# A two-layer encoder trunk on one core: the beginning put into a written order behind products of zeros, a mixer's normalisation moved by two steps, and another last block

## The chip, the cores and the metric

The kernel runs on one core of one Trainium2 chip. Its time is the device time of one execution in microseconds (us). PE is TensorE with its weight loads as PEld, DVE is VectorE, ACT is ScalarE, POOL is GpSimd, SP is SyncE, which issues most DMAs.

## What is computed

512 tokens of 1024 channels pass two layers. Layer 0 mixes by a short gated convolution beside latent attention, which share one input projection; layer 1 by a convolution module (gate, depthwise convolution of width 31, LayerNorm, swish, projection). Each layer ends with a squared-ReLU MLP of hidden width 4096. Every sub-layer is wrapped in two RMS norms:

```python
x = x + rms_norm(m, g[1])
h = rms_norm(x, g[2])
x = x + rms_norm(squared_relu_mlp(h, mlp_w1[i], mlp_w2[i]), g[3])
```

## The kernel before

Activations lie with channels on the 128 partitions, so 1024 channels are eight chunks of 128 x 512 tokens. Products are in float32 split in two float32r parts, a high part (`hi`) and what is left of it (`lo`): each product of a chunk is three matmuls, hi*hi, hi*lo and lo*hi, and one 128-column block of an output (a **block** below) is 24 of them into one PSUM bank. Weights come in **strips** of 128 x 1024: `strip` (line 210) loads one (SP), ACT casts its high part `whi` (L223), POOL subtracts to get `wlo` (L224). A strip passes through one of two raw buffers (more in later phases) into one of eight pairs of `whi` and `wlo`. PSUM has eight banks: three named `S`, two `pj`, one `o`, two `mi`.

The **beginning** (`START`, `split_x`, lines 564 to 600): for each chunk of x, SP loads it, DVE scales it by its gain (L572), ACT rounds it to `h` (L230), DVE subtracts the low part (L233). ACT squares the chunks (L358), DVE adds the squares (L333), PE sums them over partitions (L368), DVE makes the reciprocal root in 14 small instructions (`rstd`, L394 to L424), PE spreads it over the partitions (`spread`, L433) and ACT puts it into `R0` (L600). Only with `R0` can DVE empty a block's bank (L608). Five blocks (`latent`) need it, twelve and one more follow. Here the framework's scheduler orders all engines. The first transfer of all is `gtok`, a row of gains for the last norm, on the ACT queue (L1133).

From layer 0's MLP on (`M2`) the tokens go in two halves, A and B, and a list of steps is the program: `up` and `down` are the MLP's two products, `pw1` and `pw2` the convolution module's, `norm` its LayerNorm, `join` a residual with its norms. The numbers of a step are layer, quarter of the hidden width, and first and last block. DVE runs in the order in which the steps are issued; the scheduler orders the other engines. The convolutions are DVE instructions (L832) that `fill(us)` puts between the steps, as many as the step's worth in `FILL` pays. Steps of a chain (`norm`, `join`) are long runs of dependent instructions, and `hold` and `pace` put steps of the other half between them, taken from the list until one of the same half comes. `norm A` first uses up what is left of A's convolutions, a step for each 1.96 us of them; then it takes the mean (L847), subtracts it (L856), squares and adds (L333), makes the root, spreads it, multiplies (L864), and ACT applies the swish and rounds to `h`, on which `pw2 A` waits.

The **end** (`end_step`): the last two 128-token blocks b of half B are made with tokens on partitions, in two halves f of 512 channels; the last bank (b 1, f 1) in two parts of 256 columns. `piece` adds what was kept (L1029), squares on ACT with a sum (L1031), multiplies by the gain on POOL (L1032); `root` adds the sums and runs `rstd`; `leave` does the last multiply-add (L1051) and stores.

Of the kernel before, what the change touches and what calls it, by code (L numbers as in the profile page):

```python
# [37 lines left out]
OP_US, STEP_US = 0.39, 2.35  # L40
TAP_US = {T // 2: (0.395, 0.525)}
FILL = {'up': 2.3, 'down': 2.3, 'first': 2.6, 'sum': 1.8, 'pw1': 4.8, 'pw2': 2.3}
START = ['x', (128,), 'x', (256, 512, 768), 'x', 'x', 'x', 'x', 'x', 'x', ()]
ADD0 = 0
LAG = 4
MULT_POOL = (0, 0, 0, 0, 0, 0, 0, 3)
W0 = True
WHOLE = (True,) * 5
# [82 lines left out]
def trunk(ctx: ExitStack, tc: tile.TileContext, a, out: bass.AP, out_b: bass.AP):  # L131
# [310 lines left out]
    def gains(layer, n):  # L442
        return V_GAIN + (layer * 4 + n) * NC
# [123 lines left out]
    s0 = Sum(NC, FULL, nc.gpsimd if ADD0 else nc.vector, whole=W0)

    def split_x(j):
        load_x(xs[j], j)  # L570
        t, (hi, lo) = scratch(T), (h.t[:, :T] for h in hs[j])
        nc.vector.tensor_scalar(out=t, in0=xs[j].t, scalar1=col(gains(0, 0) + j), scalar2=None, op0=ALU.mult)  # L572
        settle()
        split((hi, lo), t, nc.vector, late=late)
        if j >= LAG:
            s0.square(xs[j - LAG].t)

    win, j = [], 0
    for what in START:
        if what == "x":  # L580
            split_x(j)
            j += 1
        else:
            win.append(strip(a["win"][len(win)], cuts=what))
    nc.sync.dma_start(kst, a["consts"])
    nc.sync.dma_start(vec[:, V_QN:], a["vecs"][:, V_QN:])
    settle()
    for j in range(NC - LAG, NC):
        s0.square(xs[j].t)
        settle()  # L590
# [9 lines left out]
    nc.scalar.activation(R0, spread(rstd(s0.done(STARTS), D, inverse=inv0)[:, :NB]), AF.Copy)  # L600


    def latent(m0, n, gain, slot):
        lat, ss = [], Sum(n, FULL, whole=WL)
        for j in range(n):
            acc = linear(win[m0 + j] if m0 + j < len(win) else strip(a["win"][m0 + j]), hs)
# [408 lines left out]
    def end_step(tok, h, layer, g):  # L1015

        f12 = lack.pop(h)
        banks_step(h, g)
        ws = []
        for k in range(NC):  # L1020
            ws.append(take())
            issue([turn_mm(turned[0, f][0], h, ws[k], k, 0, slice(0, T), f * T) for f in range(2)])
            settle()
        parts = {b: [] for b in range(2)}

        def piece(b, f, cols):
            acc, m, _ = turned[b, f]
            acc, m, g = acc[:, cols], m[:, cols], turned["gain"][:, f * T + cols.start : f * T + cols.stop]
# [6 lines left out]
        def root(b):  # L1035
            s = misc()[:, :1]
            p = parts[b]
            if len(p) == 3:
                nc.vector.scalar_tensor_tensor(
                    out=s, in0=p[0], scalar=p[1], in1=p[2], op0=ALU.add, op1=ALU.add  # L1040
                )
            else:
                nc.vector.tensor_tensor(out=s, in0=p[0], in1=p[1], op=ALU.add)
            return rstd(s, D, tuple(f[:, b : b + 1] for f in f12))

        def leave(b, r, n):
            w = T // n
            for f in range(2):
                for i in range(n):
                    m, x = (t[:, i * w : i * w + w] for t in turned[b, f][1:])  # L1050
                    nc.vector.scalar_tensor_tensor(  # L1051
                        out=x, in0=m, scalar=r, in1=x, op0=ALU.mult, op1=ALU.add
                    )
                    q = nc.scalar if i % 2 else nc.sync
                    q.dma_start(out_b[b * P : (b + 1) * P, f * T + i * w : f * T + i * w + w], x)
# [204 lines left out]
```

## Time and profile before

| | |
|---|---|
| three runs, median | 1172.47 us (1171.79 to 1172.93) |
| the profiled execution's own time | 1173.47 us |
| its span, first to last instruction | 1171.7 us |
| PE busy | 1134.6 us (97%) |
| POOL, ACT, DVE busy | 846.0, 661.5, 649.2 us |
| mean granted TensorE clock | 0.993 |

The span is 1.8 us shorter than the execution's time; the rest is start and stop around it. A share of busy time is a mean over stages, so PE's idle time is best looked for stage by stage.

### The profile page before, as it was taken

What the parts mean: (1) busy time and instruction counts of PE and PEld (TensorE: products, weight loads), DVE (VectorE), ACT (ScalarE), POOL (GpSimd) and SP (SyncE); (2) the same over time, 40 slices, a digit from 0 to 9 for tenths busy, and PEclk for the clock granted to TensorE, in tenths of its full rate; (3) what the DMA queues carried; (4) which work ended last, traced back from release to release, by engine and by line L of the source; (5) the groups of instructions that cost most, each with busy time, mean ns of one, the idle gap of its engine ahead of it and who ended that gap; (6) DMA issues with size and microseconds to landing.
All of it is one profiled execution on the core that took longest, in us unless ns stands there. A gap on an engine that the chain in (4) does not pass through costs nothing.

```text
span 1171.7 us, 22121 instructions
## 1 busy us (share of the span) xinstructions
PE 1134.6 (97%) x8492; PEld 1081.3 (92%) x8492; DVE 649.2 (55%) x1693; ACT 661.5 (56%) x1211; POOL 846.0 (72%) x408
## 2 busy tenths in 40 slices
PE   7999989999999999999999999999999999999996
PEld 5778778999999999999999999999999999898895
DVE  5672699455432222669996364589995254131134
ACT  5431677456744445744655686745566776455451
POOL 5663563148878778688898578789787878779881
PEclk9999999999999999999999899999999999999999
DMA  6421332027545555545565355556555545565530
GB/s 222 154 90 30 106 100 72 1 92 235 201 161 182 178 180 169 174 163 181 180 216 187 122 196 181 179 171 207 169 195 178 180 163 180 165 231 182 179 108 36
DMA packets 55257, 184.47 MB, mean 157 GB/s; under 512 B 6384, under 2 KB 10352, under 8 KB 55152
## 3 DMA queue, kind: packets, MB, share of 16 engines
q1 hardware_dynamic: 54576, 182.02, 46.9%
q8 instruction: 66, 1.08, 0.4%
q10 hardware_dynamic: 576, 1.05, 0.3%
q14 instruction: 39, 0.32, 0.1%
HBM read 180.94 MB, written 2.10 MB: 156 GB/s over the span
## 4 chain that ended last, share of the span: by engine, by line
PE 85%; DVE 6%; ACT 3%; DMA 3%; POOL 1%; issue 1%; SPq 0%; DVEq 0%; ACTq 0%; POOLq 0%
PE S L246 20%; PE S L247 19%; PE S L248 19%; PE pj L246 5%; PE pj L247 5%; PE pj L248 5%; PE pj L990 4%; PE S L990 4%; DMA raw<-in_win 2%; POOL wlo L224 1%; ACT whi L223 1%; DVE pr L767 1%; DMA raw<-in_w 1%; PE mi L433 1%; PE mi L770 1%
## 5 line engine op out<-in xcount | busy, mean ns | idle before, releaser
L224 POOL TENSOR_TENSOR wlo<-raw,whi 128x1024 fp32r<-128x1024 f32 (+2 forms) x347 | 802.0, 2327 | 263.2 <-ACT whi L223 243.6
L223 ACT ACTIVATE whi<-raw 128x1024 fp32r<-128x1024 f32 (+2 forms) x347 | 356.6, 1033 | 368.7 <-PE S L247 173.3
L246 PE MATMUL S<-h,whi 128*128 128x256 f32 (+3 forms) x1208 | 347.7, 291 | 5.0 <-ACT h L230 2.9
L247 PE MATMUL S<-h,whi 128*128 128x256 f32 (+3 forms) x1208 | 349.0, 290 | 0.0
L248 PE MATMUL S<-h,wlo 128*128 128x256 f32 (+3 forms) x1208 | 348.7, 289 | 0.0
L246 PEld LDWEIGHTS S<-h,whi 128*128 128x128 f32 x1208 | 229.0, 191 | 10.1 <-ACT h L230 3.4
L247 PEld LDWEIGHTS S<-h,whi 128*128 128x128 f32 x1208 | 230.5, 191 | 3.5 <-issue 0.2
L248 PEld LDWEIGHTS S<-h,wlo 128*128 128x128 f32 x1208 | 230.5, 191 | 3.3 <-POOL wlo L224 0.3
L832 DVE SCALAR_TENSOR_TENSOR pj<-u,taps,pj 128x256 f32<-128x256 f32 x464 | 192.6, 484 | 1.3
L246 PE MATMUL S<-hid,whi 128*128 128x256 f32 (+2 forms) x664 | 185.3, 281 | 1.4 <-DVE acc L333 1.2
L248 PE MATMUL S<-hid,wlo 128*128 128x256 f32 (+2 forms) x664 | 186.5, 282 | 0.0
L247 PE MATMUL S<-hid,whi 128*128 128x256 f32 (+2 forms) x664 | 186.3, 281 | 0.0
L246 PEld LDWEIGHTS S<-hid,whi 128*128 128x128 f32 x664 | 124.8, 189 | 2.5 <-DVE acc L333 1.8
L248 PEld LDWEIGHTS S<-hid,wlo 128*128 128x128 f32 x664 | 125.3, 189 | 0.0
L247 PEld LDWEIGHTS S<-hid,whi 128*128 128x128 f32 x664 | 125.3, 189 | 0.0
L246 PE MATMUL pj<-h,whi 128*128 128x256 f32 (+3 forms) x344 | 105.5, 307 | 9.5 <-ACT h L230 7.6
L248 PE MATMUL pj<-h,wlo 128*128 128x256 f32 (+3 forms) x344 | 105.3, 306 | 0.3 <-POOL wlo L224 0.3
L247 PE MATMUL pj<-h,whi 128*128 128x256 f32 (+3 forms) x344 | 105.3, 306 | 0.0
L246 PEld LDWEIGHTS pj<-h,whi 128*128 128x128 f32 x344 | 65.5, 191 | 12.4 <-ACT h L230 7.6
L236 DVE TENSOR_TENSOR hid<-S,hid 128x256 fp32r<-128x256 f32 (+2 forms) x102 | 42.9, 420 | 52.7 <-ACT hid L230 52.2
L247 PEld LDWEIGHTS pj<-h,whi 128*128 128x128 f32 x344 | 65.5, 190 | 3.4 <-DVE h L233 1.1
L248 PEld LDWEIGHTS pj<-h,wlo 128*128 128x128 f32 x344 | 65.6, 191 | 3.1 <-POOL wlo L224 0.7
(267 smaller groups left out, 1740.2 us busy)
## 6 DMA issues: line engine op xcount, KB each, us to landing
raw<-in_w SPq DMA_DIRECT2D x224, 512.0 KB, 3.3
raw<-in_pw SPq DMA_DIRECT2D x48, 512.0 KB, 3.3
raw<-in_w2t SPq DMA_DIRECT2D x32, 512.0 KB, 3.3
raw<-in_win SPq DMA_DIRECT2D x16, 512.0 KB, 3.3
x<-in_xT SPq DMA_DIRECT2D x16, 256.0 KB, 4.4
raw<-in_wout SPq DMA_DIRECT2D x8, 512.0 KB, 3.3
raw<-in_wq SPq DMA_DIRECT2D x8, 192.0 KB, 2.4
out<-x SPq DMA_DIRECT2D x8, 128.0 KB, 3.5
```

The costliest lines, as they stand in the source:

```text
L223: nc.scalar.activation(h, r, AF.Copy)
L224: nc.gpsimd.tensor_tensor(out=lo[:, c0:c1], in0=r, in1=h.bitcast(F32), op=ALU.subtract)
L236: eng.tensor_tensor(out=lo, in0=src, in1=hi.bitcast(F32), op=ALU.subtract)
L246: nc.tensor.matmul(acc, sh, mh, start=i == 0, stop=False)
L247: nc.tensor.matmul(acc, sh, ml, start=False, stop=False)
L248: nc.tensor.matmul(acc, sl, mh, start=False, stop=i == n - 1)
L433: nc.tensor.matmul(o[:, sl], r[:, b : b + 1].to_broadcast([bw, P]), ident[:bw, :bw], start=True, stop=True,)
L767: eng.tensor_scalar(out=pr_, in0=pr_, scalar1=sm, scalar2=None, op0=ALU.mult)
L770: nc.tensor.transpose(tp[:, kb * P : (kb + 1) * P], pr_[:, kb * P : (kb + 1) * P], ident)
L832: nc.vector.scalar_tensor_tensor(out=dst, in0=src, scalar=wk, in1=acc, op0=ALU.mult, op1=ALU.add)
L990: nc.tensor.matmul(acc, x, w, start=start, stop=stop)
```

## The change

1. **The beginning** is written out by hand inside a manual schedule of PE, DVE and ACT. PE starts with 12 products of a tile of zeros into a bank that nothing reads, does chunk 0 of block 0, 10 more products of zeros, chunk 0 of block 1, and then every chunk for blocks 0 and 1 as it comes; block 2 as a whole, the sums for `R0`, six chunks of block 3. DVE scales one chunk ahead of the subtraction. Squares and their sum come later.
2. `gtok` is loaded at the banks of the turned steps, on SP's queue.
3. **The list**: in layer 0, `norm A` stands two `up` steps of B later (after block 4 of quarter 2), and `pw2 A` and `join A` two `up` steps later (after block 2 of quarter 3).
4. `fill` is paid by the step's width (272, 240 or 256 tokens, over 256).
5. **The end**: the second part of the last bank gets a bank of its own (`S`); the gain is multiplied on DVE into PSUM; the sum over earlier pieces is made beforehand (`near`); `root` has nine small instructions on SBUF tiles in place of 16; the stores of the last block are of 512, 256 and 256 columns and not four of 256.

```diff
-M2 = [... ('up', 'B', 0, 2, 0, 2), ('norm', 'A'), ('up', 'B', 0, 2, 2, 8), ('down', 'B', 0, 2, 0, 8), ('pw2', 'A', 0, 8), ('join', 'A', 1, 1), ('up', 'B', 0, 3, 0, 8), ('down', 'B', 0, 3, 0, 8), ...]
+M2 = [... ('up', 'B', 0, 2, 0, 4), ('norm', 'A'), ('up', 'B', 0, 2, 4, 8), ('down', 'B', 0, 2, 0, 8), ('up', 'B', 0, 3, 0, 2), ('pw2', 'A', 0, 8), ('join', 'A', 1, 1), ('up', 'B', 0, 3, 2, 8), ('down', 'B', 0, 3, 0, 8), ...]
...
-START = ['x', (128,), 'x', (256, 512, 768), 'x', 'x', 'x', 'x', 'x', 'x', ()]
...
+    with tc.manual_schedule(engines={E.PE, E.DVE, E.Activation}):
+        idle, bank = tmp("tq", F32R), ps("S")
+        nc.vector.memset(idle.bitcast(F32), 0.0)
+        def busy(n):
+            for _ in range(n):
+                nc.tensor.matmul(bank, idle[:, :P], idle, start=True, stop=True)
...
+        def bit(i, k):
...
+            nc.tensor.matmul(accs[i], wh[:, kk], x_h, start=k == 0, stop=False)
+            nc.tensor.matmul(accs[i], wl[:, kk], x_h, start=False, stop=False)
+            nc.tensor.matmul(accs[i], wh[:, kk], x_l, start=False, stop=k == NC - 1)
+        busy(12)
...
+        scale_x(0)
+        win.append(strip(a["win"][0], cuts=(128,)))
+        rest_x(0)
+        bit(0, 0)
+        busy(10)
+        scale_x(1)
+        win.append(strip(a["win"][1], cuts=(256, 512, 768)))
+        bit(1, 0)
+        for j in range(2, NC + 1):
+            if j < NC:
+                scale_x(j)
+            if j >= 5:
+                square_x(j - 5)
+            rest_x(j - 1)
+            bit(0, j - 1)
+            bit(1, j - 1)
+        win.append(strip(a["win"][2]))
...
+        for j in range(1, NC):
+            if j + 3 < NC:
+                square_x(j + 3)
+            if j == 4:
+                win.append(strip(a["win"][3]))
+            last = add_x(j)
+        for k in range(NC):
+            bit(2, k)
+        win.append(strip(a["win"][4]))
...
+        root = rstd(s0.done(STARTS), D, inverse=inv0)[:, :NB]
+        for k in range(NC - 2):
+            bit(3, k)
+        nc.scalar.activation(R0, spread(root), AF.Copy)
+        for k in range(NC - 2, NC):
+            bit(3, k)
...
-        fill(FILL["up"])
+        fill(FILL["up"] * seg.w / 256)
...
-            turned["gain"] = gtok
+            nc.sync.dma_start(gtok, a["gain"].to_broadcast([P, D]))
...
-            nc.scalar.activation(acc, m, AF.Square, accum_out=sm)
-            nc.gpsimd.tensor_tensor(out=m, in0=m, in1=g, op=ALU.mult)
+            nc.scalar.activation(ps("o")[:, : acc.shape[-1]], m, AF.Square, accum_out=sm)
+            nc.vector.tensor_tensor(out=acc, in0=m, in1=g, op=ALU.mult)
...
         for i in range(2):
             cols = slice(i * T // 2, (i + 1) * T // 2)
-            rest(1, cols)
-            piece(1, 1, cols)
-        leave(1, root(1), 2)
+            acc = (ps("S") if i else turned[1, 1][0])[:, : T // 2]
+            rest(1, cols, acc)
+            if i:
+                fd, v = near(1)
+            piece(1, 1, cols, acc)
+        leave(1, root(1, fd, v))
...
-    nc.scalar.dma_start(gtok, a["gain"].to_broadcast([P, D]))
```

The new `scale_x`, `rest_x`, `square_x` and `add_x` hold the instructions of `split_x` and of the squares, one each; `add_x` adds into the bank `o`.

Three places show what moves. The first is the beginning of PE's queue: `S_109` is the bank of zeros, `pj` and `S` are blocks 0 and 1, `h` pairs are chunks of x. Before, then now:

```order
L246 MATMUL pj_231<-h_88,whi_109 128x512
L247 MATMUL pj_231<-h_89,whi_109 128x512
L248 MATMUL pj_231<-h_88,wlo_110 128x512
L246 MATMUL S_264<-h_88,whi_123 128x512
L247 MATMUL S_264<-h_89,whi_123 128x512
L246 MATMUL pj_231<-h_90,whi_109 128x512
```

```order
L580 MATMUL S_109<-tq_108 128x512 x12
L590 MATMUL pj_138<-h_88,whi_129 128x512
L591 MATMUL pj_138<-h_88,wlo_130 128x512
L592 MATMUL pj_138<-h_89,whi_129 128x512
L580 MATMUL S_109<-tq_108 128x512 x10
L590 MATMUL S_171<-h_88,whi_157 128x512
L591 MATMUL S_171<-h_88,wlo_158 128x512
L592 MATMUL S_171<-h_89,whi_157 128x512
```

Products of zeros stand ahead of the first real one and between chunk 0 of block 0 and of block 1, and a low weight part is now asked for one product earlier.

The second is PE's queue where `norm A` ends: `mi_7868` and `mi_7928` are its sums of squares, `mi_7918` and `mi_7998` the root spread, `S_7892` the last `down` of quarter 2, `S_8007` the second `up` of quarter 3, and `h_2181` and `h_2210` the first chunk that `pw2 A` reads. Before, then now:

```order
L247 MATMUL S_7892<-hid_7270,whi_7705 128x240
L248 MATMUL S_7892<-hid_7269,wlo_7706 128x240
L368 MATMUL mi_7868<-kst,acc_7742 128x1 x2
L433 MATMUL mi_7918<-kst,s_7872 128x128 x2
L246 MATMUL S_7967<-h_2181,whi_7756 128x256
```

```order
L243 MATMUL S_8007<-h_2220,whi_7816 128x240
L365 MATMUL mi_7928<-kst,acc_7802 128x1 x2
L244 MATMUL S_8007<-h_2221,whi_7816 128x240
L245 MATMUL S_8007<-h_2220,wlo_7817 128x240
L243 MATMUL S_8007<-h_2222,whi_7816 128x240
L244 MATMUL S_8007<-h_2223,whi_7816 128x240
L245 MATMUL S_8007<-h_2222,wlo_7817 128x240
L243 MATMUL S_8007<-h_2224,whi_7816 128x240
L244 MATMUL S_8007<-h_2225,whi_7816 128x240
L245 MATMUL S_8007<-h_2224,wlo_7817 128x240
L430 MATMUL mi_7998<-kst,s_7932 128x128 x2
L243 MATMUL S_8117<-h_2210,whi_7897 128x256
```

Two whole `up` blocks now stand between the last `down` and `pw2 A`; eight products of the second lie behind the sums, none behind the spread.

The third is DVE's queue at the same place, from the last small instruction of the root on (`hid` are the low parts of the two `up` blocks). Before, then now:

```order
L419 SCALAR_TENSOR_TENSOR s_7872<-mi_7868,s_7872 128x2
L535 TENSOR_TENSOR m_2164<-S_7892,m_2164 128x240
L864 TENSOR_TENSOR m_2157<-m_2157,mi_7918 128x256
L864 TENSOR_TENSOR m_2158<-m_2158,mi_7918 128x256
L864 TENSOR_TENSOR m_2159<-m_2159,mi_7918 128x256
```

```order
L416 SCALAR_TENSOR_TENSOR s_7932<-mi_7928,s_7932 128x2
L233 TENSOR_TENSOR hid_7947<-S_7968,hid_7946 128x240
L233 TENSOR_TENSOR hid_7949<-S_8007,hid_7948 128x240
L919 TENSOR_TENSOR m_2186<-m_2186,mi_7998 128x256
L919 TENSOR_TENSOR m_2187<-m_2187,mi_7998 128x256
L919 TENSOR_TENSOR m_2188<-m_2188,mi_7998 128x256
```

The subtractions of both `up` blocks stand in DVE's fixed order ahead of the normalisation's multiplications.

## Rows read from the trace of the kernel before

**Rows 1.** The page: PE's line (busy us, share of the span, instructions), and the chain that ended last, by engine.

```profile
PE 1134.6 (97%) x8492; PEld 1081.3 (92%) x8492; DVE 649.2 (55%) x1693; ACT 661.5 (56%) x1211; POOL 846.0 (72%) x408
...
PE 85%; DVE 6%; ACT 3%; DMA 3%; POOL 1%; issue 1%; SPq 0%; DVEq 0%; ACTq 0%; POOLq 0%
```

**Rows 2.** The span in stretches of 25 us, ahead of them one of 4 us in the beginning: the stretch, its length, then busy us (and instructions) of PE, PEld, DVE, ACT and POOL, then the granted clock as a share of 2.4 GHz, the DMA engines' busy share and GB/s.

```profile
4.00:8.00 4.00, 0.39 (x1) 0.29 (x1) 1.17 (x2) 1.87 (x4) 0.45 (x1) 1.00 1.00 371
...
0.00:25.00 25.00, 17.13 (x62) 12.73 (x63) 13.08 (x21) 15.43 (x26) 11.13 (x13) 1.00 0.69 238
...
50.00:75.00 25.00, 24.54 (x114) 19.70 (x113) 23.27 (x48) 10.71 (x13) 16.08 (x10) 1.00 0.33 106
...
625.00:650.00 25.00, 20.25 (x165) 19.70 (x164) 15.16 (x50) 15.02 (x27) 18.98 (x8) 0.88 0.53 174
650.00:675.00 25.00, 25.00 (x196) 25.00 (x195) 5.45 (x14) 16.41 (x31) 16.64 (x7) 0.91 0.38 126
...
1150.00:1175.00 25.00, 11.52 (x72) 10.04 (x70) 11.52 (x41) 3.08 (x10) 5.27 (x5) 0.85 0.12 42
```

**Rows 3.** The timeline of the first 15 us: start, duration (both us), engine (q: its queue), line, operation, out<-in, count, and in brackets the idle time before it and what ended it.

```profile
0.73 0.42 ACTq L1133 DMA_DIRECT2D gtok<-in_gain  x1
...
1.17 0.42 SPq L207 DMA_DIRECT2D x<-in_xT  x1
...
6.17 0.75 DVE L572 TENSOR_SCALAR mi<-x,vec 128x512 f32<-128x512 f32 x1 [5.31 <-DMA x<-in_xT]
...
7.00 0.45 POOL L224 TENSOR_TENSOR wlo<-raw,whi 128x128 fp32r<-128x128 f32 x1 [6.56 <-ACT whi L223]
...
7.61 0.80 PE L246 MATMUL pj<-h,whi 128*128 128x512 f32 x1 [7.61 <-ACT h L230]
...
8.47 4.89 POOL L224 TENSOR_TENSOR wlo<-raw,whi 128x896 fp32r<-128x896 f32 x5 [1.02 <-ACT whi L223]
...
9.36 0.63 PE L246 MATMUL S<-h,whi 128*128 128x512 f32 x1
...
9.78 0.63 PE L247 MATMUL S<-h,whi 128*128 128x512 f32 x1
...
13.22 0.68 DVE L233 TENSOR_TENSOR h<-o,h 128x512 fp32r<-128x512 f32 x1
...
13.82 0.68 DVE L233 TENSOR_TENSOR h<-mi,h 128x512 fp32r<-128x512 f32 x1
13.92 0.39 PE L246 MATMUL pj<-h,whi 128*128 128x512 f32 x1
...
14.15 0.39 PE L247 MATMUL S<-h,whi 128*128 128x512 f32 x1
```

**Rows 4.** The same view from 17 to 52 us: the third strip, the root for `R0`, and what waits for it.

```profile
17.44 4.76 POOL L224 TENSOR_TENSOR wlo<-raw,whi 128x1024 fp32r<-128x1024 f32 x2 [4.08 <-ACT whi L223]
17.79 1.06 ACT L223 ACTIVATE whi<-raw 128x1024 fp32r<-128x1024 f32 x1
...
33.93 0.17 DVE L394 TENSOR_SCALAR mi<-mi 128x6 f32<-128x6 f32 x1 [5.27 <-PE mi L368]
...
36.33 0.15 DVE L424 TENSOR_TENSOR inv<-mi,s 128x6 f32<-128x6 f32 x1
...
39.52 1.05 PE L433 MATMUL mi<-kst,s 128*128 128x128 f32 x8
...
40.68 0.58 ACT L600 ACTIVATE R<-mi 128x512 f32<-128x512 f32 x1
...
41.29 0.69 DVE L608 TENSOR_TENSOR ycat<-pj,R 128x512 f32<-128x512 f32 x1 [4.80 <-ACT R L600]
...
42.04 0.50 PE L246 MATMUL pj<-h,whi 128*128 128x512 f32 x1 [1.47 <-DVE ycat L608]
...
48.89 0.74 DVE L238 SCALAR_TENSOR_TENSOR m<-ycat,vec,m 128x512 fp32r<-128x512 f32 x1
49.56 2.89 DVE L238 SCALAR_TENSOR_TENSOR x<-ycat,vec,x 128x512 fp32r<-128x512 f32 x1
```

**Rows 5.** The timeline of PE where `norm A` ends and `pw2 A` begins.

```profile
641.35 0.28 PE L248 MATMUL S<-hid,wlo 128*128 128x240 f32 x1
642.15 0.58 PE L368 MATMUL mi<-kst,acc 128*128 128x1 f32 x4 [0.53 <-DVE acc L333]
645.04 1.22 PE L433 MATMUL mi<-kst,s 128*128 128x128 f32 x4 [2.32 <-DVE s L419]
...
648.17 1.01 PE L246 MATMUL S<-h,whi 128*128 128x256 f32 x3 [1.91 <-ACT h L230]
```

**Rows 6.** The stretches around it, columns as in rows 2, and one of the attention.

```profile
644.00:648.00 4.00, 1.22 (x4) 0.93 (x4) 2.23 (x9) 1.24 (x3) 1.07 (x1) 0.51 0.70 242
648.00:652.00 4.00, 3.83 (x18) 3.83 (x19) 3.52 (x11) 3.97 (x11) 0.00 (x0) 0.50 0.00 0
652.00:656.00 4.00, 4.00 (x27) 4.00 (x27) 1.24 (x4) 1.23 (x4) 0.00 (x0) 0.71 0.00 0
656.00:660.00 4.00, 4.00 (x36) 4.00 (x35) 0.00 (x0) 3.18 (x6) 2.04 (x1) 1.00 0.00 0
140.00:160.00 20.00, 16.65 (x96) 13.57 (x95) 19.60 (x36) 14.66 (x30) 15.46 (x9) 1.00 0.39 129
```

**Rows 7.** PE's waits over the whole span: who waited for whom, us in total, times, the longest.

```profile
PE mi L770 <- DVE pt L236: 1.8, 1, 1.8
```

**Rows 8.** The timeline of the last 32 us.

```profile
1159.44 0.38 PE L990 MATMUL pj<-whi,hid 128*128 128x256 f32 x1 [1.06 <-ACT pj L1031]
...
1162.68 0.42 DVE L1029 TENSOR_TENSOR u<-pj,u 128x256 f32<-128x256 f32 x1 [3.83 <-PE pj L990]
...
1163.68 0.79 DVE L1039 SCALAR_TENSOR_TENSOR mi<-s,s,s 128x1 f32<-128x1 f32 x1 [0.58 <-ACT pj L1031]
...
1164.50 0.17 DVE L391 TENSOR_TENSOR mi<-mi,fB 128x1 f32<-128x1 f32 x1
1164.70 0.17 DVE L394 TENSOR_SCALAR mi<-mi 128x1 f32<-128x1 f32 x1
...
1167.22 1.67 DVE L1051 SCALAR_TENSOR_TENSOR u<-u,s,u 128x256 f32<-128x256 f32 x4
```

**Rows 9.** Two dependent DVE instructions on SBUF, the first of one column (attention).

```profile
178.07 0.17 DVE L765 RECIPROCAL s<-s 128x1 f32<-128x1 f32 x1
178.27 1.86 DVE L767 TENSOR_SCALAR pr<-pr,s 128x512 f32<-128x512 f32 x1
```

More of the change, by code (lines that the diff above doesn't have):

```diff
@@ L42 @@
 FILL = {'up': 2.3, 'down': 2.3, 'first': 2.6, 'sum': 1.8, 'pw1': 4.8, 'pw2': 2.3}
-START = ['x', (128,), 'x', (256, 512, 768), 'x', 'x', 'x', 'x', 'x', 'x', ()]
-ADD0 = 0
-LAG = 4
 MULT_POOL = (0, 0, 0, 0, 0, 0, 0, 3)
@@ L565, in trunk @@
     hs = [hpair() for _ in range(NC)]
[L567 to L590, printed above, removed]
     def spread_sb(r):
@@ L603, in latent @@
+    scope["turn"] = 3
     def latent(m0, n, gain, slot):
@@ L605, in latent @@
         for j in range(n):
-            acc = linear(win[m0 + j] if m0 + j < len(win) else strip(a["win"][m0 + j]), hs)
+            acc = accs[m0 + j] if m0 + j < len(accs) else linear(win[m0 + j], hs)
             t = tmp("ycat")
@@ L905, in down_step @@
         )
-        fill(FILL["sum" if last else "down" if g else "first"])
+        fill(FILL["sum" if last else "down" if g else "first"] * seg_of(h, layer).w / 256)
     def shared_step(tok, h, src, seg, first, m):
@@ L1024, in end_step, with piece @@
         parts = {b: [] for b in range(2)}
-        def piece(b, f, cols):
-            acc, m, _ = turned[b, f]
-            acc, m, g = acc[:, cols], m[:, cols], turned["gain"][:, f * T + cols.start : f * T + cols.stop]
+        scaled = {b: [] for b in range(2)}
+        def piece(b, f, cols, acc=None):
+            bank, m, x = turned[b, f]
+            acc = bank[:, cols] if acc is None else acc
+            m, x, g = m[:, cols], x[:, cols], gtok[:, f * T + cols.start : f * T + cols.stop]
             nc.vector.tensor_tensor(out=m, in0=acc, in1=m, op=ALU.add)
@@ L1030, in piece @@
             sm = small(1)
-            nc.scalar.activation(acc, m, AF.Square, accum_out=sm)
-            nc.gpsimd.tensor_tensor(out=m, in0=m, in1=g, op=ALU.mult)
+            nc.scalar.activation(ps("o")[:, : acc.shape[-1]], m, AF.Square, accum_out=sm)
+            nc.vector.tensor_tensor(out=acc, in0=m, in1=g, op=ALU.mult)
             parts[b].append(sm)
[L1035 to L1055, printed above, removed]
@@ L1057, in rest, with near @@
-        def rest(f, cols):
+            scaled[b].append((acc, x, f * T + cols.start))
+        def near(b):
+            fd, v = small(1), small(1)
+            nc.vector.tensor_scalar(
+                out=fd, in0=f12[1][:, b : b + 1], scalar1=1.0 / D, scalar2=None, op0=ALU.mult
+            )
+            v0 = parts[b][0]
+            for p in parts[b][1:]:
+                nc.vector.tensor_tensor(out=v0, in0=v0, in1=p, op=ALU.add)
+            nc.vector.tensor_scalar(out=v, in0=v0, scalar1=fd, scalar2=EPS, op0=ALU.mult, op1=ALU.add)
+            return fd, v
@@ new lines, in root @@
+        def root(b, fd, v):
+            nc.vector.scalar_tensor_tensor(
+                out=v, in0=parts[b][-1], scalar=fd, in1=v, op0=ALU.mult, op1=ALU.add
+            )
+            r, y, q, out = (small(1) for _ in range(4))
+            nc.vector.tensor_scalar(
+                out=r.bitcast(I32), in0=v.bitcast(I32), scalar1=-0.5, scalar2=float(0x5F3759DF),
+                op0=ALU.mult, op1=ALU.add,
+            )
+            nc.vector.scalar_tensor_tensor(out=y, in0=r, scalar=v, in1=r, op0=ALU.mult, op1=ALU.mult)
+            nc.vector.tensor_scalar(out=q, in0=y, scalar1=0.375, scalar2=-1.25, op0=ALU.mult, op1=ALU.add)
+            nc.vector.tensor_scalar(out=q, in0=q, scalar1=y, scalar2=1.875, op0=ALU.mult, op1=ALU.add)
+            nc.vector.tensor_tensor(out=r, in0=q, in1=r, op=ALU.mult)
+            nc.vector.scalar_tensor_tensor(out=y, in0=r, scalar=v, in1=r, op0=ALU.mult, op1=ALU.mult)
+            nc.vector.tensor_scalar(out=q, in0=y, scalar1=-0.5, scalar2=1.5, op0=ALU.mult, op1=ALU.add)
+            nc.vector.scalar_tensor_tensor(
+                out=out, in0=q, scalar=r, in1=f12[0][:, b : b + 1], op0=ALU.mult, op1=ALU.mult
+            )
+            return out
@@ L1058, in rest, with leave @@
+        def leave(b, r):
+            for i, (m, x, c) in enumerate(scaled[b]):
+                nc.vector.scalar_tensor_tensor(out=x, in0=m, scalar=r, in1=x, op0=ALU.mult, op1=ALU.add)
+                q = nc.scalar if i % 2 else nc.sync
+                q.dma_start(out_b[b * P : (b + 1) * P, c : c + x.shape[-1]], x)
+        def rest(f, cols, acc=None):
+            acc = turned[1, f][0][:, cols] if acc is None else acc
+            n = f * T + cols.start
             for k in range(NC):
-                issue([turn_mm(turned[1, f][0], h, ws[k], k, 1, cols, f * T)])
+                issue([turn_mm(acc, h, ws[k], k, 1, slice(0, cols.stop - cols.start), n)])
@@ L1061, in end_step @@
         for f in range(2):
             piece(0, f, slice(0, T))
+            if f == 0:
+                fd, v = near(0)
         rest(0, slice(0, T))
-        r = root(0)
-        leave(0, r, 1)
+        leave(0, root(0, fd, v))
         piece(1, 0, slice(0, T))
```

31 lines of the change are left out of this document (29 added, 2 removed).

## The prediction

> **What bounds the kernel now.** I read the page first: PE is busy 97% of the span and carries 85% of the chain that ended last [rows 1]. So an edit pays only where PE has nothing to do, or runs slowly. The stretches of 25 us, read next, show where that is: most have PE busy for 25.00; those that have not, or have a granted clock under 1.00, lie mainly at the beginning, at 625 to 675 (0.88 and 0.91) and at the end [rows 2]. The change touches just these three places, so the timeline of each was read for the wait that ends last there.
>
> *Beginning.* The first product stands at 7.61 and is released by the rounded chunk `h`, behind x's landing, on which DVE waited 5.31 us [rows 3]. [...] PE gets half speed somewhere between 7.61 and 13.92. At the other end, PE finishes its five blocks at 39.52, only then spreads the root that DVE had at 36.48 (36.33 + 0.15), and starts the sixth block at 42.04, 1.47 us of it idle behind DVE's first use of `R0` [rows 4].
>
> *`norm A`.* The last dense product is at 641.35, the next at 648.17 [rows 5]. Between them stand sums, a wait of 2.32 for the root, the spread, and 1.91 for the first `h`. Then the clock falls to 0.51 and 0.50 and is back at 1.00 after 656 [rows 6].
>
> *End.* PE waits 1.06 for ACT's square, which reads the bank that the second part reuses; then small instructions from 1163.68 to 1167.22 keep the output waiting [rows 8].
>
> **The sum, part by part.**
>
> *Beginning.* `gtok` (128 x 1024 floats, 0.52 MB) is issued at 0.73, ahead of x at 1.17 [rows 3]. The DMA engines are full, at 371 GB/s, from 4 to 8 us [rows 2], so without it the first transfers land about 0.52 MB / 371 GB/s = 1.4 us sooner: DVE's first scaling at 4.8 and not 6.17, the first real product possible at 6.2. Zeros: PE can begin them once DVE has cleared their tile, which I put at 1.5 (the engines' first instructions are at about 1). 12 x 0.42 = 5.1, so 6.6; they cost the real product 0.4. What they buy is that the products behind them are 0.23 apart. The ten more zeros (2.3 us) fill the wait for block 1's first low quarter: POOL made it in before at 7.00 + 0.45, a wait, then 2.1 for 896 columns and 0.65 for a quarter (by width, of 4.89 for all five), so about 11.3 [rows 3]; now about 10.2. Then 45 to 48 products x 0.23 = 10.4: blocks 0 and 1 are complete at 20.5. DVE must deliver a chunk in each 6 x 0.23 = 1.38 us and needs at most 0.75 for a scaling and 0.60 for a subtraction (13.22 to 13.82), 1.35 [rows 3], which just suffices. The third strip's cast now stands behind the eighth rounding and four squares on ACT: about 18.0 + 1.06, and POOL's 2.4, give 21.4 (before: 17.79) [rows 4]. PE idles 1 us there. Block 2 takes 24 x 0.23 = 5.5, to 26.9; six sums 0.7; 32 products 7.3, to 34.9. The root's 2.6 us (33.93 to 36.48 in [rows 4]) lie beside these. The spread is half of 1.05, then ACT 0.58, DVE 0.69: the first bank is free at 36.7, while 16 products last until 39.1. The sixth block starts there and not at 42.04: **-2.9**. DVE gets `R0` 5 us earlier, so PE's 0.46 us of idle time at 50 to 75 [rows 2] should go: -0.5. Together **-3.4**. Bounds: nothing but the 1.47 of the wait is won, -1.0 with a strip late; or all of 42.04 - 39.1, the later idle and the 1 us behind the third strip, and a little more of the clock, -5.5.
>
> *`norm A`.* Two more `up` blocks are 48 products. 36 fill 4 us after 656 [rows 6]: 0.11 each, 5.3 us. They fill the gap from 641.46 on, but the same chain still hangs behind: the sums come only 8 products (0.9 us) before the blocks' end; from sums to spread it took 645.04 - 642.15 = 2.9, so PE idles 2.0; the spread 0.6 (half of 1.22), and from its end to the first product of `pw2` 648.17 - 646.26 = 1.9 [rows 5]. That makes 4.5 us almost without products, where there were 6.7: -2.2. DVE has two subtractions more ahead of the multiplications; both blocks end before the spread, so they are done in time. Whether the clock still falls decides the rest. After the hole 18 and 27 products ran in 8 us [rows 6] where the full clock does 36 in 4: 72 - 45 = 27 products x 0.11 = 3.0 us. No row decides. After a gap of 1.8 with PE idle (the `mi` of [rows 7]) the clock in that stretch stayed at 1.00 [rows 6]; after 6.7 it fell. Mine is two gaps of 2 with a little between. I take the middle, -1.2, less than half since the nearest row is of one gap and not two: **-3.4** in all, bounds -1.8 and -5.2. `join A` then has the six `up` steps and the `down` steps of quarter 3, which is enough: no new hole. That narrower steps pay less for convolutions moves DVE work that has cover (DVE 55% [rows 1]): nothing, bounds +-0.5.
>
> *End.* The bank of its own: -1.06 [rows 8]. The root: 3.5 us from 1163.68 to 1167.22 become one instruction of about 0.8 (0.79, with the wait behind an ACT result) and eight of 0.20 (1164.50 to 1164.70 on PSUM [rows 8]; 178.07 to 178.27 on SBUF [rows 9], the same): 2.4 to 2.5, -1.0. DVE's gain multiplication (0.42 as its addition) hides beside ACT's square, for which DVE waited 0.58. Three last multiply-adds in place of four: 1.67 becomes about 1.35, -0.3. Sum **-2.4**; bounds -1.5 (reading a bank costs more) and -3.2.
>
> [...]
>
> Sum: -3.4 - 3.4 - 2.4 = -9.2. The profiled execution took 1173.47, which gives 1164.3; the median of the runs lies 1.0 below it: **1163.3**.
>
> **Rivals.**
>
> 1. *The beginning gains nothing.* A third strip later than 21.4, or DVE held up: the same operation takes 0.74 in one row and 2.89 in the next [rows 4], where POOL subtracts beside it. If a scaling or subtraction of a chunk takes that, PE waits at once, since 1.35 of 1.38 leaves no slack. For: POOL works through seven pieces there. Against: the subtractions 0.60 apart [rows 3] stand beside POOL's work too. -3.4 - 2.4: 1166.7 (1172.47 - 5.8). [...]
> 2. *The hole hardly shrinks.* The clock falls as before, and the waits are 0.5 longer: -1.7 there. -3.4 - 1.7 - 2.4 = -7.5: 1165.0. With 1 as well: 1168.4. If the second half of the chain is also late, -6: 1166.5.
> 3. *Slower: the zeros do not raise the clock.* The record reads 1.00 where products are 0.42 apart, so what raised it before 13.92 may be real data. Then the ten zeros cost 4.2 and not 2.3, and 48 products run 0.42 apart: +48 x 0.19 + 1.9 = +11. The beginning turns from -3.4 to +7.6, the whole to +1.8: 1174.3; with `norm A` at its poor end 1176. It decides from 48 products x (9.2 - 1.9)/9.1, or about 38 of them at half speed. For: no row shows PE on zeros. Against: it rose in the middle of products on x's data, which have nothing special, while PE did nothing else [rows 3]. [...]
> 4. *It does not do what it says:* `gtok` still comes in the beginning, since SP's order puts it behind the third strip. That is behind x, so the first product gains; the fourth strip may then be 1.4 later, but is needed only at 27. Nothing.
>
> **How the numbers follow.** Forecast 0.63; rival 1 0.13; rival 2 0.10; both, near 1169, 0.05; rival 3 0.04; the rest, unnamed, 0.05. About 0.2% (2.3 us) is what a measurement of this kernel can tell from no change. All but both-together with bad luck, rival 3 and half of the rest are below 1170.1: faster 0.89, same 0.06, slower 0.05. The forecast's own range, with the bounds of its terms, is 1158.5 to 1166; rivals 1 and 2 stretch it to **1158.5 to 1168.5**, which leaves some 0.15 out.
>
> **What would show it.** In the changed profile: zeros 0.42 apart and all real products 0.23 apart from about 6.6; first scaling at 4.8; PE's wait before block 2 about 1 us; sixth block at 39. At `norm A` two gaps of 2 us, and the clock of the 4 us behind them between 0.5 and 1. At the end no wait of PE for ACT, 2.5 us from the first small instruction to the output. It is wrong if real products stand 0.42 apart beyond 8 us, if the sixth block starts after 41, or if less than 2 us are won around 640.

## The result, and the profile after

The changed kernel takes **1165.83 us** (median, 1164.71 to 1166.98) where the kernel before took 1172.70 on the same chip: a ratio of 0.9939 (0.9923 to 0.9954), 6.9 us less. Forecast were 1163.3 and 9.2 us less, with a range of 1158.5 to 1168.5. The spans of the two profiled executions are 7.9 us apart (1171.7 and 1163.8).

Where they lie was read by counting PE's products: the n-th product of the program, zeros left out, starts 2.1 us earlier at 67 us, 1.6 earlier at 220, 2.6 at 628, 5.1 at 680, and the last one 6.4 earlier; the rest of the 7.9 lies behind the last product.

First the page: PE and the chain by engine (as rows 1), then three stretches (as rows 2).

```profile
PE 1136.4 (98%) x8514; PEld 1084.1 (93%) x8514; DVE 651.0 (56%) x1690; ACT 662.5 (57%) x1212; POOL 841.6 (72%) x403
...
PE 91%; DVE 3%; ACT 2%; DMA 1%; issue 1%; POOL 1%; SPq 0%; DVEq 0%; ACTq 0%; POOLq 0%
```

```profile
0.00:25.00 25.00, 21.22 (x82) 16.44 (x83) 16.30 (x25) 14.66 (x26) 9.89 (x12) 1.00 0.65 217
...
50.00:75.00 25.00, 25.00 (x114) 20.47 (x114) 19.39 (x46) 9.93 (x11) 17.74 (x11) 1.00 0.43 144
...
625.00:650.00 25.00, 21.51 (x186) 21.03 (x185) 13.83 (x46) 16.41 (x30) 21.69 (x10) 0.93 0.60 196
```

Of the chain, DVE's 6% and ACT's and DMA's 3% have become 3, 2 and 1. The stretch from 50 to 75 is full; the one at 625 still has 3.5 us without PE and a clock of 0.93.

The timeline of the beginning (columns as in rows 3):

```profile
1.48 4.62 PE L580 MATMUL S<-tq 128*128 128x512 f32 x12 [1.48 <-DVE tq L576]
...
3.98 0.75 DVE L601 TENSOR_SCALAR mi<-x,vec 128x512 f32<-128x512 f32 x1 [2.55 <-DMA x<-in_xT]
...
5.94 0.40 PE L590 MATMUL pj<-h,whi 128*128 128x512 f32 x1
...
6.17 0.48 PE L591 MATMUL pj<-h,wlo 128*128 128x512 f32 x1
...
10.53 0.50 PE L591 MATMUL S<-h,wlo 128*128 128x512 f32 x1 [0.82 <-POOL wlo L221]
...
18.90 1.05 ACT L220 ACTIVATE whi<-raw 128x1024 fp32r<-128x1024 f32 x1
...
20.03 2.39 POOL L221 TENSOR_TENSOR wlo<-raw,whi 128x1024 fp32r<-128x1024 f32 x1 [7.46 <-ACT whi L220]
...
22.47 0.50 PE L591 MATMUL pj<-h,wlo 128*128 128x512 f32 x1 [1.45 <-POOL wlo L221]
...
27.82 1.39 PE L365 MATMUL mi<-kst,ycat 128*128 128x1 f32 x12
29.08 0.48 PE L590 MATMUL S<-h,whi 128*128 128x512 f32 x1
...
36.42 1.05 PE L430 MATMUL mi<-kst,s 128*128 128x128 f32 x8
...
37.23 0.48 PE L590 MATMUL S<-h,whi 128*128 128x512 f32 x1
...
40.98 0.39 PE L243 MATMUL pj<-h,whi 128*128 128x512 f32 x1
```

DVE scales at 3.98 where it scaled at 6.17, and the first real products stand 0.23 apart, as those at 13.92 did before [rows 3], behind zeros alone. The zeros themselves stand 0.43 apart up to 4.6 us and 0.23 from 5.0 on. Then PE waits 1.45 for the third strip's low part, cast at 18.90. The sixth block starts at 40.98; it was 42.04 [rows 4].

`norm A` (as rows 5 and 6) and the end (as rows 8):

```profile
646.19 0.82 PE L430 MATMUL mi<-kst,s 128*128 128x128 f32 x4 [1.31 <-DVE s L416]
649.18 1.01 PE L243 MATMUL S<-h,whi 128*128 128x256 f32 x3 [2.18 <-ACT h L227]
```

```profile
644.00:648.00 4.00, 1.69 (x12) 1.21 (x11) 3.10 (x17) 2.29 (x5) 3.25 (x2) 0.83 0.70 238
648.00:652.00 4.00, 2.82 (x13) 2.82 (x14) 3.23 (x10) 3.97 (x11) 0.33 (x1) 0.50 0.40 136
652.00:656.00 4.00, 4.00 (x30) 4.00 (x30) 1.94 (x5) 2.24 (x6) 0.00 (x0) 0.82 0.01 4
```

```profile
1156.17 0.42 DVE L1086 TENSOR_TENSOR u<-S,u 128x256 f32<-128x256 f32 x1 [1.38 <-PE S L1045]
...
1157.23 0.22 DVE L1107 SCALAR_TENSOR_TENSOR s<-s,s,s 128x1 f32<-128x1 f32 x1 [0.17 <-ACT o L1088]
1157.49 0.15 DVE L1111 TENSOR_SCALAR s<-s 128x1 int32<-128x1 int32 x1
...
1159.26 0.75 DVE L1128 SCALAR_TENSOR_TENSOR u<-S,s,u 128x512 f32<-128x512 f32 x1
```

The two gaps came near the forecast (PE idle for 1.31 and 2.18), and the granted clock was 0.50 from 648 to 652 all the same. At the end the small instructions take 2.03 us (1157.23 to 1159.26); they took 3.54 [rows 8].

### The profile page after: what moved, and what is told of

It reads as the page before. It is cut to its first block, busy times and chain, and to the rows that moved or that the text cites. A ratio compares the mean times of both kernels' runs of the same rounds, so it can differ in the third digit from the quotient of the medians.

```text
span 1163.8 us, 22171 instructions
## 1 busy us (share of the span) xinstructions
PE 1136.4 (98%) x8514; PEld 1084.1 (93%) x8514; DVE 651.0 (56%) x1690; ACT 662.5 (57%) x1212; POOL 841.6 (72%) x403
## 4 chain that ended last, share of the span: by engine, by line
PE 91%; DVE 3%; ACT 2%; DMA 1%; issue 1%; POOL 1%; SPq 0%; DVEq 0%; ACTq 0%; POOLq 0%
PE S L243 21%; PE S L244 21%; PE S L245 21%; PE pj L243 5%; PE pj L244 5%; PE pj L245 5%; PE S L1045 4%; PE pj L1045 4%; DVE pr L822 1%; DMA raw<-in_win 1%; ACT whi L220 1%; PE mi L365 1%; POOL wlo L221 1%; PE mi L430 1%; PE mi L825 1%
## 5 line engine op out<-in xcount | busy, mean ns | idle before, releaser
L243 PE MATMUL S<-h,whi 128*128 128x256 f32 (+3 forms) x1200 | 343.8, 290 | 5.2 <-ACT h L227 3.2
L244 PE MATMUL S<-h,whi 128*128 128x256 f32 (+3 forms) x1200 | 345.7, 289 | 0.0
L243 PE MATMUL S<-hid,whi 128*128 128x256 f32 (+2 forms) x672 | 187.8, 281 | 2.0 <-DVE acc L330 2.0
L244 PE MATMUL S<-hid,whi 128*128 128x256 f32 (+2 forms) x672 | 188.6, 281 | 0.0
L243 PEld LDWEIGHTS S<-hid,whi 128*128 128x128 f32 x672 | 126.5, 189 | 3.0 <-DVE acc L330 2.6
L244 PEld LDWEIGHTS S<-hid,whi 128*128 128x128 f32 x672 | 126.8, 189 | 0.0
L243 PE MATMUL pj<-h,whi 128*128 128x256 f32 (+3 forms) x320 | 95.6, 299 | 0.3 <-DVE h L230 0.3
L244 PE MATMUL pj<-h,whi 128*128 128x256 f32 (+3 forms) x320 | 95.7, 299 | 0.0
L245 PE MATMUL pj<-h,wlo 128*128 128x256 f32 (+3 forms) x320 | 95.5, 298 | 0.0
L243 PEld LDWEIGHTS pj<-h,whi 128*128 128x128 f32 x320 | 60.9, 190 | 2.1 <-DVE h L230 0.6
L245 PEld LDWEIGHTS pj<-h,wlo 128*128 128x128 f32 x320 | 60.9, 190 | 1.8 <-issue 0.2
L244 PEld LDWEIGHTS pj<-h,whi 128*128 128x128 f32 x320 | 60.8, 190 | 1.8 <-issue 0.2
```

Of the source, the lines that this page charges most:

```text
L243: nc.tensor.matmul(acc, sh, mh, start=i == 0, stop=False)
L244: nc.tensor.matmul(acc, sh, ml, start=False, stop=False)
L245: nc.tensor.matmul(acc, sl, mh, start=False, stop=i == n - 1)
```

## The experiments

Each time stands beside the kernel before on the same chip. That was 1174.4 beside the first four runs, 1174.1 beside the next four and 1172.8 beside the last four, so ratios are compared, and a stage is read from its trace.

**The end alone** (gtok stays first):

```diff
+            acc = (ps("S") if i else turned[1, 1][0])[:, : T // 2]
+            nc.vector.tensor_tensor(out=acc, in0=m, in1=g, op=ALU.mult)
+        leave(1, root(1, fd, v))
```

> The kernel before with the end of the change alone (own bank for the second part, gain multiplied on DVE, nine small instructions in place of 16); gtok stays first. Theory (the three places are won one by one, and what the changed profile shows at the end, -2.7, belongs to the end): PE's wait of 1.06 before the last part goes, the small instructions take 2.4 and not 3.5, the last multiply-adds 1.4 and not 1.7: 1172.6 becomes 1169.9, with nothing moved before 1140 us. Rival (part of those 2.7 us came from the other half running ahead after the earlier edits): -1.3, 1171.3.

Measured 1170.91, ratio 0.9976 (0.9964 to 0.9988), 2.8 us. In its trace the last product moves by 1.3 against those at 1140 us and the end of the span by 1.4 more: 2.7, as in the changed kernel. The theory holds. Ahead of 1140 us, where the edit changes nothing, products still stand between 1.4 us later and 0.3 sooner than in the profile of the kernel before: so far apart are two executions with PE and DVE in the same order.

**The list alone:**

```diff
-... ('up', 'B', 0, 2, 0, 2), ('norm', 'A'), ..., ('down', 'B', 0, 2, 0, 8), ('pw2', 'A', 0, 8), ...
+... ('up', 'B', 0, 2, 0, 4), ('norm', 'A'), ..., ('up', 'B', 0, 3, 0, 2), ('pw2', 'A', 0, 8), ...
```

> The kernel before with the changed list of steps alone. Theory: the hole at norm A shrinks as in the changed kernel, 6.7 us without products to 4.5 with the 8 products' rest, and the clock still falls, so -2.6: 1170.0. Rival A (paying the fill by width, which moves DVE's convolutions, is what lets norm A end in time): less than -1 here, over 1171.6. Rival B (the clock stays up when the gap is alone): -4, 1168.6.

Measured 1172.27, 0.9981 (0.9970 to 0.9992), 2.2 us. The size is near the theory's, the shape is not: one gap of 3.2 us behind the spread, and none ahead of it. That pointed to the fill (below).

**No zeros:** `range(n)` in `busy` becomes `range(0)`.

> The changed kernel without its 22 products of zeros; everything else in the same order. Theory (they only hold the clock up, and 1.6 us of what they win is lost again before block 2, which waits for the third strip): about a dozen real products run 0.42 apart, 2.3 us, of which the wait before block 2 takes back 1.6, so the sixth block starts 0.5 to 1.5 later than 40.9 and the time is about 1166.8. Rival A (the clock does not matter there, x's landing and DVE set the pace): no change, 1165.8. Rival B (the zeros carry the whole gain of the beginning): +2.5 or more, 1168.3.

Measured 1166.67, 0.9941 (0.9917 to 0.9964), the changed kernel's ratio. Here the clock does rise late:

```profile
13.66 0.63 PE L592 MATMUL S<-h,whi 128*128 128x512 f32 x1
14.09 0.60 PE L590 MATMUL pj<-h,whi 128*128 128x512 f32 x1
14.52 0.41 PE L591 MATMUL pj<-h,wlo 128*128 128x512 f32 x1
14.76 0.39 PE L592 MATMUL pj<-h,whi 128*128 128x512 f32 x1
```

Products are 0.43 apart until 14.5. Yet the sixth block starts at 41.10, only 0.12 later: the wait before block 2 had 1.5 us to give back. The zeros of the changed kernel bought nothing.

**gtok first again:**

```diff
+    nc.scalar.dma_start(gtok, a["gain"].to_broadcast([P, D]))
...
-            nc.sync.dma_start(gtok, a["gain"].to_broadcast([P, D]))
```

> The changed kernel with gtok's load at 0.7 us on the ACT queue again, as in the kernel before. Theory from the landings (x's first chunk at 3.87 and not 6.07, but its last at 13.30 and not 14.10, the third strip at 15.37 and not 15.88): only 0.5 to 0.8 us of the stream is gtok's, so the sixth block moves by about +0.6, 1166.4. Rival (the prediction's 0.52 MB at the full rate): +1.4 or more, 1167.2.

Measured 1167.51, ratio 0.9942 (0.9924 to 0.9961), not told apart from the changed kernel by times; in the trace every product from the sixth block to `norm A` is 1.1 to 1.3 later, twice what the theory said and nearer the rival. DVE's first scaling, in the ten profiles with gtok late, stands at 3.97 to 4.21; with gtok first at 6.17, 6.48, 7.38 and 7.48. So that one transfer costs 2.0 to 3.5 us at the first chunk, and not the same in each execution.

**The clock in norm A's gaps, both filled:**

```diff
+                nc.tensor.matmul(side[:, T // 2 :], scope["v"][:, :1].to_broadcast([P, P]), kst[:, : T // 2], start=True, stop=True)
...
+                for _ in range(GAP[1]):
+                    nc.tensor.matmul(scope["bank"][:, T // 2 :], ident, v, start=True, stop=True)
```

> The changed kernel with products that nothing reads in norm A's two gaps: three 128x256 ones that hang on the root's first copy, four that hang on the first normalised chunk. Theory (the clock falls because PE has nothing to do, and any product holds it up, as the zeros of the beginning did): pw2 A's first products run 0.12 apart at once, where 14 to 28 of them ran 0.21 apart in the five profiles so far, so 1.5 to 2.7 us are won: about -2 against the changed kernel, 1163.8 against its 1165.8. Rival A (only the products of the program count, or two short fillings are not enough): 14 to 28 products still 0.21 apart, no gain. Rival B (they come in the way of the chain): the first product of pw2 later than 2.6 us behind the spread, slower.

Measured 1165.78, 0.9930 (0.9915 to 0.9945). `pw2 A`'s products run 0.12 apart soon after its first ones, but the first stands at 651.02, 7.0 us behind the last dense product (4.5 in the changed kernel):

```profile
645.52 2.46 PE L387 MATMUL mi<-kst,s 128*128 128x256 f32 x6 [1.32 <-DVE s L429]
647.78 1.06 PE L444 MATMUL mi<-kst,s 128*128 128x128 f32 x4
649.35 2.03 PE L936 MATMUL mi<-m,kst 128*128 128x256 f32 x8 [0.51 <-DVE m L933]
651.02 0.70 PE L246 MATMUL S<-h,whi 128*128 128x256 f32 x3
```

```profile
644.00:648.00 4.00, 2.68 (x10) 2.05 (x10) 1.95 (x10) 2.06 (x4) 2.92 (x2) 0.75 0.55 183
```

Rival B holds: the three products waited for the end of the root (`s`, 1.32), not its first copy, and pushed the spread back by 2.3 us. In the code they write into the bank in which the root is still being made. The theory is borne out for the second gap alone: while the first gap's products ran, the granted clock of the stretch was 0.75, and the spread's products stand 0.21 apart. In this profile `norm A` costs 1.9 us more than in the changed kernel; the ratios do not tell the two kernels apart.

**The third strip's cast earlier**, and the same **without zeros**:

```diff
             nc.vector.tensor_scalar(out=t, in0=xs[j].t, ...)
+            if j == 7:
+                win.append(strip(a["win"][2]))
             nc.scalar.activation(hs[j][0].t[:, :T], t, AF.Copy)
...
+            if j == 7:
+                square_x(1)
-            if j >= 5:
+            if j >= 5 and j != 6:
                 square_x(j - 5)
...
-        win.append(strip(a["win"][2]))
```

> The changed kernel with the third strip's cast between the seventh and the eighth rounding on ACT, three squares later. Theory (PE's wait of 1.6 before block 2 is this strip's chain alone, cast, subtraction, and takes back what was won ahead of it): the wait goes, the eighth rounding is 0.2 later, and the sixth block starts 1.2 to 1.4 sooner than 40.9; all of it lasts to the end: 1164.5 where the changed kernel has 1165.8. Rival A (the sum of squares, now three squares later, becomes the wait): PE waits for the sums instead, gain under 0.4. Rival B (the bank or a later strip takes the gain back before 60 us): under 0.4 too, but with block 2 early.

> As the run before (third strip's cast earlier), and without the 22 products of zeros. Theory (the zeros bought nothing because PE waited at block 2 anyway; with that wait gone they must pay): 18 real products 0.42 apart, of which the chunk's pace hides some, so block 2 starts 0.9 later than with zeros and the time is about 0.9 longer, 1165.4. Rival (DVE and x's landing pace PE in any case): no difference to the run before.

Measured 1163.75, 0.9912 (0.9895 to 0.9928), and without zeros 1166.88, 0.9937 (0.9922 to 0.9952): 3.1 us apart. With the earlier cast (16.81, not 18.90) the sums and the sixth block of the two kernels are:

```profile
17.95 2.41 POOL L221 TENSOR_TENSOR wlo<-raw,whi 128x1024 fp32r<-128x1024 f32 x1 [5.57 <-ACT whi L220]
...
26.15 1.39 PE L365 MATMUL mi<-kst,ycat 128*128 128x1 f32 x12
...
39.30 0.39 PE L243 MATMUL pj<-h,whi 128*128 128x512 f32 x1
```

```profile
28.41 1.39 PE L365 MATMUL mi<-kst,ycat 128*128 128x1 f32 x12
...
41.59 0.50 PE L243 MATMUL pj<-h,whi 128*128 128x512 f32 x1
```

The wait is gone, the sixth block 1.7 sooner than in the changed kernel, and 1.7 is still there at the last product. And now the zeros pay: 2.3 us, more than the 0.9 expected, since the pace of the chunks hid none of it. The same zeros are worth nothing or 2.3 us, by what waits next.

**The fill by 256 tokens for every step:** `* seg.w / 256` removed in `up_step` and `down_step`.

> The changed kernel with the convolutions paid by 256 tokens for every step, as before, not by the step's width. Theory from the run with the list alone (there the gap at norm A was 3.2 us in one piece and none ahead of the spread): the hole is again about 1 us shorter, and 0.9 comes back as waits between 660 and 700 us, so no change within 0.5: 1165.8. Rival (the width makes the whole of norm A later and nothing else): 1 us faster, 1164.8.

Measured 1164.75, 0.9921 (0.9906 to 0.9936). Its ratio is not told apart from the changed kernel's (0.9939). In the trace 1.3 us is won at `norm A`, and the last product stands 0.9 sooner: the rival.

```profile
640.83 0.50 PE L365 MATMUL mi<-kst,acc 128*128 128x1 f32 x4
644.96 0.61 PE L430 MATMUL mi<-kst,s 128*128 128x128 f32 x4
648.49 0.79 PE L243 MATMUL S<-h,whi 128*128 128x256 f32 x2 [2.93 <-ACT h L227]
```

With less pay for narrow steps, `norm A` finds more convolutions left and draws one block more ahead of its sums. In the changed kernel only eight products stay behind them; here the 4 us from sums to spread are full.

**Both of these together, and products in the second gap alone** (as before, four of them, nothing ahead of the spread):

> The changed kernel with the third strip's cast earlier and the convolutions paid by 256 tokens for every step. Theory (the two are in different places and add): -1.7 from the beginning and -0.9 from norm A against the changed kernel, 1163.2 where the two single runs gave 1163.75 and 1164.75. Rival (one of the two was a disturbance of its profile): only 1164 to 1165.

> The run before with four products that nothing reads in the gap behind the spread, hanging on the first normalised chunk; nothing in front of the spread. Theory (in the earlier run with both gaps filled the clock stayed up, and what was lost came from the three products that stood ahead of the spread and waited for the end of the root): the chain keeps its time, pw2 A's first products run at 0.12, 1.0 us is won, the chunk's pace taking the rest of 1.6: 1162.2. Rival (the clock falls in the 1 us that stays empty ahead of them, or they end too late): as the run before, 1163.2.

Measured 1163.24, 0.9915 (0.9902 to 0.9929), and 1162.58, 0.9918 (0.9904 to 0.9931). Neither is told apart from the earlier cast alone by its ratio. The stage shows what was meant: `norm A` loses 5.0 us in the first (6.2 in the changed kernel), 4.3 in the second, whose clock never falls there:

```profile
644.00:648.00 4.00, 2.54 (x14) 1.94 (x12) 1.64 (x5) 3.15 (x8) 2.98 (x2) 1.00 0.41 137
648.00:652.00 4.00, 4.00 (x30) 3.64 (x31) 3.24 (x10) 3.87 (x11) 0.00 (x0) 1.00 0.39 131
```

Only 0.7 comes of it, since PE at full clock waits 0.94 for the next `h`. That wait is of the filling's own making. First DVE's multiplications in the run without it, then the four products, DVE and PE in the run with it:

```profile
644.53 1.08 DVE L922 TENSOR_TENSOR m<-m,mi 128x256 f32<-128x256 f32 x3 [0.62 <-PE mi L430]
```

```profile
644.75 1.99 PE L927 MATMUL mi<-m,kst 128*128 128x256 f32 x8 [0.51 <-DVE m L924]
...
646.78 0.75 DVE L924 TENSOR_TENSOR m<-m,mi 128x256 f32<-128x256 f32 x2 [2.09 <-PE mi L927]
...
647.92 0.39 PE L244 MATMUL S<-h,whi 128*128 128x256 f32 x1 [0.94 <-DVE h L230]
```

The four products (two records each) write into the bank from which DVE reads the spread root, and DVE's second multiplication waits 2.09 for them; without them three multiplications ran back to back. Products into a bank outside the chain were not tried. The first product of `pw2 A` also stands 2.8 behind the spread's start and not 3.5, so how much of the 0.7 is the clock's is not shown. And both kernels lose 0.9 elsewhere, in the attention, at an order of PE and DVE that is the same in the kernel with the cast alone (last section). In their own stages the two edits add as expected; the time, which meets the expected 1163.2, has this loss in it and so does not show that.

**gtok late alone, and the beginning alone**, on the kernel before:

> The kernel before with gtok's load moved to the banks of the turned steps and nothing else; the scheduler's order changes a little with it. Theory (at the beginning most of what is won is this one transfer, since the changed kernel with gtok first started its sixth block no sooner than the kernel before): x's first chunk at about 3.9, the sixth block 1.0 to 2.0 sooner than in profiles with gtok first (42.8 to 44.2), and -1.5 at the end: 1172.6 on the first chip, -1.5 against before here. Rival (without the written order PE waits for the scheduler's order of chunks and weights, and the time is lost again): less than -0.5.

> The kernel before with the new beginning alone (written order, zeros, gtok late). Theory: as in the changed kernel, block 2 waits 1.6 for its strip, the sixth block starts at about 41, R0 is 4 to 5 us sooner and the stretch to 55 us gains 1 more: -2.5 to -3.5 against before, about 1.5 more than gtok alone. Rival (gtok late is all): the same as the run before within 0.5.

Measured 1171.03, 0.9985 (0.9976 to 0.9994), and 1170.51, 0.9983 (0.9974 to 0.9992). First scalings at 4.01 and 4.06, sixth blocks at 40.84 and 40.87 (first gtok late alone, then the beginning):

```profile
4.01 0.75 DVE L572 TENSOR_SCALAR mi<-x,vec 128x512 f32<-128x512 f32 x1 [3.14 <-DMA x<-in_xT]
...
40.84 0.50 PE L246 MATMUL pj<-h,whi 128*128 128x512 f32 x1 [0.72 <-DVE ycat L608]
```

```profile
4.06 0.75 DVE L603 TENSOR_SCALAR mi<-x,vec 128x512 f32<-128x512 f32 x1 [2.63 <-DMA x<-in_xT]
...
40.87 0.39 PE L246 MATMUL pj<-h,whi 128*128 128x512 f32 x1
```

At 67 us the second is 0.4 ahead. Against before they are -1.8 and -2.3: the first theory holds, and for the second its rival (gtok late is all) is the nearer. By medians and traces the written order, the scaling ahead and 22 zeros add half a microsecond to what one moved DMA wins, and the ratios do not tell that from nothing; with the third strip's cast earlier too, the same beginning starts its sixth block at 39.30.

## Why the prediction was right, and where it was not

The sign, the three places and the end were right; the time lies in the range. The gain was 2.3 us smaller than forecast, by four terms.

- **The beginning, -3.4 forecast.** In the pair of profiles -2.1 at 67 us. The step that failed is the sixth block at 39.1: it is 40.98. The third strip's cast is at 18.90 and not at 18.0, so block 2's wait ends 1.0 later than forecast; the sums take 1.26 (27.82 to 29.08) and not 0.7, and the spread 0.8 and not 0.5. I had put gtok at 1.4; at the first chunk it is 2.0 and more, at the sixth block 1.3, but the clock that the zeros hold up, the order and the scaling ahead are lost in front of block 2. Rival 1's mechanism (a strip later than 21.4) was half true: it came at 22.4 and took 1.0, not all. That DVE is held up did not show: the subtractions of x's chunks read one PSUM bank and one SBUF tile, and take 0.68 beside POOL's work as in [rows 3]. The instruction of 2.89 [rows 4] has two inputs in SBUF and stands beside a subtraction on POOL (49.50 to 51.89); what makes it long is not shown. The kernel's beginning also varies: with gtok first the sixth block stood at 42.04, 43.20 and 43.39 in three profiles, so the gain lies between 1.1 and 2.4 there.
- **The slower rival fell.** Behind zeros alone the clock rose: products are 0.23 apart from the first real one, where without zeros they stand 0.43 apart until 14.5. With products that nothing reads in the second gap it stayed up, at 1.00 from 648 to 652; without them it was 0.50 there in the changed kernel and 0.57 with the plain fill. That the granted clock reads 1.00 from the start, which the prediction remarks, is the record's: its first entry is the rise, at 12.59 us before and at 4.95 in the changed kernel, just where the products pass from 0.43 to 0.23 apart. The traces give this clock as a share alone, in entries of 1.00 or 0.50 before and now; the 2.4 GHz beside rows 2 is in none of them.
- **`norm A`, -3.4 forecast.** The first product of `pw2 A` stands 4.5 us behind the last dense product, as in the sum. But of the -2.2, 0.4 were sums that now stand between products and still cost their time. PE's waits fell from 4.76 (0.53, 2.32 and 1.91 [rows 5]) to 3.49 (1.31 and 2.18), -1.3, and the spread from 1.22 to 0.82. What PE lost around this place (some 40 us), over the spacing of its products at full clock, is 7.3 to 7.5 us in three profiles with the old list (8.7 in the one shown) and 5.6 to 6.9 in five of the changed kind: -1.3 rather than -3.4, -2.5 by the pair shown. The first is under the 2 us that the prediction named as a sign of being wrong. The middle taken for the clock, -1.2, was wrong: it fell in all of them, for 14 to 27 products as against 13 to 28. That the changed kernel has fewer of them in the pair shown (19 and 28) is chance, by the other profiles.
- **Pay by width, 0 forecast.** It costs 1.1 to 1.3 at just this place, 0.9 at the last product. "Moves DVE work that has cover" looked at DVE alone; what moved was how many of PE's blocks are drawn ahead of the sums. With it paid as before, the list is worth -2.3 to -2.6.
- **The end, -2.4 forecast:** -2.7. The parts: the wait (-1.3), the root (-1.5 and not -1.0, since its first instruction takes 0.22 and not 0.79), the last multiply-adds (-0.1); the stores behind them take 0.3 more. Nine small instructions stand where the trace of before has 15, not 16. They stand 0.19 to 0.26 apart on SBUF, 0.20 on PSUM [rows 8].

## What to carry to other kernels

Before pricing an edit, look at the next wait behind it: what is won ahead of a wait on another engine comes back as that wait, and the edit pays only when that is moved too (here 0 or 2.3 us for the same zeros). A load that is needed late must not be issued first: one DMA line brought most of what a rewritten beginning brought. A rule that decides how much filler is drawn ahead of a chain moves the other engines' work with it; cost it there, not on the filler's engine. Products that only hold the clock up should stay out of the banks of the chain beside them: here DVE waited 2.1 us for four of them.

## What the runs showed of the hardware

**The clock after one and the same gap is not fixed.** A gap in the attention, in which PE is idle for 1.8 us [rows 6, 7], stands in all fourteen profiles. Behind it the clock stayed at 1.00 in twelve, among them the kernel before, the changed one and the one with the cast earlier. In the two combined kernels it fell, though PE and DVE have the same order there as with the cast alone; the stretches around it, first the changed kernel, then the one with cast and fill (2.2 us ahead of it there):

```profile
146.00:150.00 4.00, 3.45 (x19) 2.60 (x17) 3.96 (x5) 3.79 (x8) 4.00 (x3) 1.00 0.13 48
150.00:154.00 4.00, 2.44 (x17) 2.05 (x18) 4.00 (x8) 1.52 (x4) 3.84 (x3) 1.00 0.35 128
```

```profile
146.00:150.00 4.00, 2.20 (x13) 1.48 (x11) 4.00 (x6) 2.00 (x3) 3.84 (x4) 1.00 0.36 131
150.00:154.00 4.00, 3.71 (x18) 3.48 (x17) 3.93 (x8) 1.64 (x4) 1.87 (x1) 0.57 0.26 80
```

It cost 0.9 us. So one trace in which the clock holds is no proof that it will in the next, and an edit's worth of under 1 us can be hidden or feigned by it. Why it fell in these two and not in the others stays open.

**The first transfers vary.** With gtok first, x's first chunk is scaled between 6.17 and 7.48 in four profiles; with gtok late, between 3.97 and 4.21.
